# A fifth 4 KB buffer for gathered expert rows in a two-layer decoder step

## The chip, the cores and the metric

The kernel runs on one core of one Trainium2 chip. The metric is the device time of one execution in microseconds (us). Before the change it was 4011.03 us, the median of three runs (4007.59 to 4016.49).

## The reference, cut to what matters

One inference step runs two decoder layers over 512 prompt positions and 32 sample positions (8 sequences of 4). The second half of each layer is a retrieval of single-neuron experts. A product-key search gives every position 8 heads of 16 expert numbers out of 16,384 with a gate for each; the position's output is a gated sum of rows of V, weighted by a dot product with rows of U:

```
a   = einsum('td,thed->the', xb, U[ib])        # rows of U, 1024 values each
wgt = gb * gelu(a)
out = einsum('the,thed->td', wgt, V[ib])       # rows of V
x   = x + out
```

Behind it stand the residual add and the RMS norm that the next layer (or the output) begins with.

## The kernel before, in words

**Two ways to the same sum.** Positions 0 to 383 (three tiles of 128) go the dense way: TensorE computes the activation of all 128 x 128 experts, a table of gates (`make_g`, line 1421 on) zeroes those that weren't chosen, and TensorE multiplies the result with all of V in the last loop of `peer`: 128 steps, each with 18 matmuls (line 1199) into six PSUM tiles. Positions 384 to 511, and the 32 sample positions, go the sparse way, by `gather` (line 1237 on): GpSimd fetches for each of 128 partitions the row of U or V that its position chose (an indirect DMA, line 1283, 128 rows of 4 KB into one buffer `g_r`), and VectorE uses it, for U with a dot product (line 1268, output `g_junk`), for V with a multiply-add into the accumulator `g_acc` (line 1276). A layer has 160 fetches of U and 160 of V, that is 320 uses on VectorE; a layer's first 128 V uses sum into the first `g_acc`, the last 32 into the second.

**Splitting.** Matmuls in float32r need each operand as a rounded high part and a rest. For a row block of V, ScalarE makes `vh` (line 98) and VectorE `vl` (line 99); for the dense weights they make `gwh` and `gwl`, for a block of U `wh` and `wl`. Step n of the last loop can't run on TensorE before its `vh`, `vl`, `gwh`, `gwl` are there.

**What sets the order around the change.** `gather` is a generator. Each call of `next` issues one fetch and, from the `GR`-th on, one use of the row that was asked for `GR - 1` calls earlier. In `make_g` the method `spend` calls it at a steady pace (a budget of 120 calls); in the last loop lines 1216 to 1218 spread the calls that are left evenly over 122 steps, and at step 123 all that is left is called, and the buffers are given back. After that come the norm of position tile 3 (`out(3, ...)`), a selection matmul on the second accumulator (line 1232), and `out` of the other tiles. The program's order is not the engines' order: a scheduler places every instruction on its engine at build time by a timeline of its own, and each engine then works through its list strictly in turn. A fetch into `g_r` waits until the use of that buffer's row before is done.

**Names.** `GR` (line 54) is the number of `g_r` buffers; lines 1279 to 1288 are the loop of `gather`. `hh` and `hl` (lines 98, 99, 181) are the next layer's inputs; in layer 0 they lie where the gather's buffers lay.

Of the kernel before, what the change touches and what calls it, by code (L numbers as in the profile page):

```python
# [50 lines left out]
GA = 4  # L51
KEEP = 6
KJ = KEEP * GA
GR = 4
APRE = 96
ROWPRE = 120
ROWSTEP = 2.5
# [22 lines left out]
class Body:  # L80
# [1156 lines left out]
    def gather(self, l, gp, acc, last):  # L1237
# [22 lines left out]
        def use(job, r):  # L1260
            nonlocal late
            which, t, s, e, w, g = job
            if late is not None and s % TOPK == 2:
                nc.vector.tensor_mul(*late)
                late = None
            if which == 0:
                jk = gp.tile([P, D], F16, name="g_junk", bufs=1)
                ins = nc.vector.scalar_tensor_tensor(jk, r, 1.0, h2t[t], op0=OP.mult, op1=OP.mult,  # L1268
                                                     accum_out=w[:, s:s + 1])
                self.tc.keep_in_program_order(ins)  # L1270
                if s % TOPK == TOPK - 1:
                    ws = w[:, s + 1 - TOPK:s + 1]
                    nc.scalar.activation(ws, ws, AF.Gelu_apprx_tanh)
                    late = (ws, ws, g[:, s + 1 - TOPK:s + 1])
            else:
                nc.vector.scalar_tensor_tensor(acc[t], r, w[:, s:s + 1], acc[t], op0=OP.mult, op1=OP.add)  # L1276

        def run():
            for n in range(len(jobs) + GR - 1):
                if n < len(jobs):  # L1280
                    which, t, s, e, w, g = jobs[n]
                    r = gp.tile([P, D], F32, name="g_r", bufs=GR)
                    nc.gpsimd.indirect_dma_start(out=r, out_offset=None,  # L1283
                                                 in_=a["v" if which else "u_rows"].rearrange("l e d -> (l e) d"),
                                                 in_offset=bass.IndirectOffsetOnAxis(ap=e[:, s:s + 1], axis=0))
                    rows.append(r)
                if n >= GR - 1:
                    use(jobs[n - GR + 1], rows.pop(0))
                yield
# [304 lines left out]
```

## Time and profile before

| | before |
|---|---|
| median of three runs | 4011.03 us |
| the profiled execution, its time | 4018.55 us |
| its span | 4016.8 us |
| TensorE matmul busy | 3798.2 us (95%) |
| VectorE busy | 2912.1 us (72%) |
| ScalarE busy | 1586.5 us (39%) |
| GpSimd busy | 1047.8 us (26%) |
| uses of U rows (line 1268) | 320, 390.3 us |
| uses of V rows (line 1276) | 320, 409.7 us |
| fetches (line 1283), U and V | 640, 936.0 us of GpSimd |
| chain that ended last | PE 79%, DVE 7%, DMA 5%, issue 5%, POOL 2% |

PE is TensorE, DVE VectorE, ACT ScalarE, POOL GpSimd, SP the engine that issues most loads. The span is the profiled stretch; the execution's time is 1.75 us longer. The profiled execution took 7.52 us more than the median. A share of busy time is a mean over stages with different limits, so the stages are read one by one.

### The profile page before, as it was taken

Reading aid. Unit: us, or ns where it says so; the run is one execution under the profiler, and the core shown is the slowest. Engines: PE = TensorE matmul, PEld = TensorE weight load, DVE = VectorE, ACT = ScalarE, POOL = GpSimd, SP = SyncE. Lnnn points to the kernel's source line nnn. Section 1 sums busy time; section 2 is a strip of 40 time slices with the busy share of each in tenths; the row PEclk is TensorE's granted clock in tenths of the full one; section 3 lists DMA queues with packets and bytes.
Section 4 is the critical chain, followed back from the end, with each engine's and each line's share of the span. In section 5 each row is a group of like instructions: output and inputs, shape, how many; then the busy total and the mean of one; then the engine's idle time right before and its main releaser. Section 6 shows DMA issues by size and latency. Waiting matters only on the chain.

```text
span 4016.8 us, 66254 instructions
## 1 busy us (share of the span) xinstructions
PE 3798.2 (95%) x25676; PEld 3426.8 (85%) x25676; DVE 2912.1 (72%) x5823; ACT 1586.5 (39%) x2377; POOL 1047.8 (26%) x880
## 2 busy tenths in 40 slices
PE   8999999999999999999679999999989989999995
PEld 7999988998898888888569998889888978888883
DVE  5554446799997878888855434568999968788887
ACT  4532333344554333333244323333455633333332
POOL 0110000004532444443511000000242224444344
PEclk9999999999999999999889999999999999999997
DMA  7243216237799999999834421361578999999997
GB/s 257 93 139 106 68 57 230 92 101 271 294 326 361 334 344 331 343 354 335 298 119 131 134 78 60 100 214 59 179 272 303 329 341 340 350 333 339 349 323 241
DMA packets 334028, 936.55 MB, mean 233 GB/s; under 512 B 28784, under 2 KB 126448, under 8 KB 330384
## 3 DMA queue, kind: packets, MB, share of 16 engines
q1 hardware_dynamic: 232912, 527.52, 38.5%
q0 software_dynamic: 92160, 335.59, 23.3%
q10 hardware_dynamic: 8640, 69.21, 4.3%
q8 instruction: 201, 3.29, 0.3%
q14 instruction: 115, 0.94, 0.1%
HBM read 835.50 MB, written 96.70 MB: 232 GB/s over the span
## 4 chain that ended last, share of the span: by engine, by line
PE 79%; DVE 7%; DMA 5%; issue 5%; POOL 2%; ACT 1%; SPq 1%; DVEq 0%; POOLq 0%; ACTq 0%
PE mm L118 34%; PE mm L1199 16%; PE sm L1199 8%; PE sm L118 7%; DMA g_r<-v,g_e 2%; POOL g_r L1283 2%; DMA g_r<-u_rows,g_e 2%; PE mm L344 2%; PE sm L586 2%; DVE wl L99 2%; PE sm L1455 1%; PE sm L1456 1%; DVE g_junk L1268 1%; PE sm L529 1%; PE sm L1340 1%
## 5 line engine op out<-in xcount | busy, mean ns | idle before, releaser
L1283 POOL DMA_INDIRECT g_r<-u_rows,g_e x320 | 488.8, 1527 | 1434.6 <-DVE g_junk L1268 706.5
L98 ACT CAST wh<-wr 128x1024 fp32r<-128x1024 f32 (+1 forms) x464 | 466.3, 1005 | 944.0 <-PE mm L118 714.9
L99 DVE TENSOR_TENSOR wl<-wr,wh 128x1024 fp32r<-128x1024 f32 (+1 forms) x464 | 541.2, 1166 | 372.1 <-ACT wh L98 363.0
L118 PE MATMUL mm<-ah,wh 128*128 128x384 f32 (+1 forms) x1792 | 597.9, 334 | 44.1 <-ACT wh L98 23.2
L118 PE MATMUL mm<-ah,wl 128*128 128x384 f32 (+1 forms) x1792 | 595.7, 335 | 27.3 <-DVE wl L99 27.2
L118 PE MATMUL mm<-al,wh 128*128 128x384 f32 (+1 forms) x1792 | 591.4, 330 | 0.5 <-DVE al L99 0.5
L1283 POOL DMA_INDIRECT g_r<-v,g_e x320 | 447.2, 1398 | 553.1 <-DVE g_acc L1276 498.9
L1276 DVE SCALAR_TENSOR_TENSOR g_acc<-g_r,g_w,g_acc 128x1024 f32<-128x1024 f32 x320 | 409.7, 1280 | 38.0 <-DMA g_r<-v,g_e 36.0
L1268 DVE SCALAR_TENSOR_TENSOR g_junk<-g_r,h2t 128x1024 f16<-128x1024 f32 x320 | 390.3, 1220 | 28.4 <-DMA g_r<-u_rows,g_e 27.5
L118 PEld LDWEIGHTS mm<-ah,wh 128*128 128x128 f32 x1792 | 341.1, 190 | 54.6 <-ACT wh L98 24.7
L118 PEld LDWEIGHTS mm<-ah,wl 128*128 128x128 f32 x1792 | 340.6, 190 | 39.0 <-DVE wl L99 38.4
L99 DVE TENSOR_TENSOR vl<-vr,vh 128x1024 fp32r<-128x1024 f32 x256 | 312.9, 1222 | 43.7 <-ACT vh L98 43.3
L118 PEld LDWEIGHTS mm<-al,wh 128*128 128x128 f32 x1792 | 341.2, 190 | 0.9 <-DVE al L99 0.9
L118 PE MATMUL mm<-hh,wl 128*128 128x272 f32 x1536 | 333.9, 294 | 0.0
L118 PE MATMUL mm<-hl,wh 128*128 128x272 f32 x1536 | 331.2, 293 | 0.0
L118 PE MATMUL mm<-hh,wh 128*128 128x272 f32 x1536 | 329.0, 294 | 0.0
L1199 PE MATMUL mm<-vl,gwh 128*128 128x512 f32 x1024 | 317.2, 391 | 0.0
L1199 PE MATMUL mm<-vh,gwl 128*128 128x512 f32 x1024 | 316.3, 390 | 0.0
L1199 PE MATMUL mm<-vh,gwh 128*128 128x512 f32 x1024 | 278.9, 391 | 1.3 <-ACT vh L98 1.1
L98 ACT CAST vh<-vr 128x1024 fp32r<-128x1024 f32 x256 | 269.3, 1053 | 4.7 <-DMA vr<-v 4.7
L118 PEld LDWEIGHTS mm<-hl,wh 128*128 128x128 f32 x1536 | 243.2, 189 | 8.4 <-issue 6.1
L118 PEld LDWEIGHTS mm<-hh,wl 128*128 128x128 f32 x1536 | 244.6, 189 | 5.5 <-issue 2.4
(478 smaller groups left out, 7378.1 us busy)
## 6 DMA issues: line engine op xcount, KB each, us to landing
vr<-v SPq DMA_DIRECT2D x256, 512.0 KB, 6.6
wr<-u SPq DMA_DIRECT2D x240, 512.0 KB, 5.4
wr<-w_in SPq DMA_DIRECT2D x96, 512.0 KB, 3.6
gd<-stage ACTq DMA_DIRECT2D x24, 1664.0 KB, 9.2
gt<-gd SPq DMA_DIRECT2D x52, 768.0 KB, 8.1
ad<-ga ACTq DMA_DIRECT2D x36, 768.0 KB, 7.3
gr<-ad SPq DMA_DIRECT2D x36, 768.0 KB, 7.9
wr<-w_o SPq DMA_DIRECT2D x32, 512.0 KB, 3.8
```

What stands on the lines that cost most here:

```text
L98: self.nc.scalar.copy(hi, src)
L99: self.nc.vector.tensor_sub(lo, src, hi.bitcast(F32))
L118: nc.tensor.matmul(o, w[:, k * P:(k + 1) * P], x[part][:, k], start=(q == 0), stop=(q == 3 * nk - 1))
L344: nc.tensor.matmul(ps[i][s][:np_], m[:, k, c], w[:, s * 512:(s + 1) * 512], start=(k == 0 and q == 0), stop=(k == NK - 1 and q == 2))
L529: nc.tensor.matmul(ps[i], x[:, k, i * P:(i + 1) * P], w[:, kk * BW:(kk + 1) * BW], start=(k == 0 and q == 0), stop=(k == NK - 1 and q == 2))
L586: self.pairs_of(lambda b, lo, hi: nc.tensor.matmul(p[lo:hi, b], w[lo:hi, b], x(b, lo, hi), start=True, stop=True))
L1199: ins = nc.tensor.matmul(po[i][s], w[:, i * P:(i + 1) * P], v[:, s * 512:(s + 1) * 512], start=(step == 1 and m == 0), stop=(step == NKEY ...
L1268: ins = nc.vector.scalar_tensor_tensor(jk, r, 1.0, h2t[t], op0=OP.mult, op1=OP.mult, accum_out=w[:, s:s + 1])
L1276: nc.vector.scalar_tensor_tensor(acc[t], r, w[:, s:s + 1], acc[t], op0=OP.mult, op1=OP.add)
L1283: nc.gpsimd.indirect_dma_start(out=r, out_offset=None, in_=a["v" if which else "u_rows"].rearrange("l e d -> (l e) d"), in_offset=bass.Ind ...
L1340: nc.tensor.matmul(ps[:, j, half], q[:, half, (i + j) * P:(i + j + 1) * P], sub[:, h * 2 + half], start=True, stop=True)
L1455: nc.tensor.matmul(ps[:, t], p_[:, w, :, half], qh[:, w, :, half], start=True, stop=False)
```

## The change

`gather` gets five buffers in place of four. A row is then asked for four calls ahead of its use; a layer's loop in `gather` has 324 calls where it had 323.

```diff
@@ -51,7 +51,7 @@
 GA = 4
 KEEP = 6
 KJ = KEEP * GA
-GR = 4
+GR = 5
 APRE = 96
 ROWPRE = 120
 ROWSTEP = 2.5
```

`GR` stands in three places: the number of buffers (`bufs=GR`), the length of the loop (`len(jobs) + GR - 1`) and the distance of use from fetch (`n >= GR - 1`). Since the scheduler places the instructions anew, their order on the engines changes too.

VectorE at the end of layer 0, from the last steps of the last loop on. `vl` and `gwl` feed TensorE's steps, line 1276 uses a V row, `hl` is the next layer's input. Before:

```order
L99 TENSOR_TENSOR vl<-vr,vh 128x1024
L173 SCALAR_TENSOR_TENSOR gr<-g_acc_14562,rs_y,gt 128x1024
L1276 SCALAR_TENSOR_TENSOR g_acc_14563<-g_r,g_w_9484,g_acc_14563 128x1024
L99 TENSOR_TENSOR gwl<-ga,gwh 128x384
L99 TENSOR_TENSOR vl<-vr,vh 128x1024
L1276 SCALAR_TENSOR_TENSOR g_acc_14563<-g_r,g_w_9484,g_acc_14563 128x1024 x28
L99 TENSOR_TENSOR hl<-sm,hh 128x4x128 x2
```

The same place with five buffers:

```order
L99 TENSOR_TENSOR vl<-vr,vh 128x1024
L99 TENSOR_TENSOR gwl<-ga,gwh 128x384
L1276 SCALAR_TENSOR_TENSOR g_acc_14561<-g_r,g_w_9484,g_acc_14561 128x1024
L99 TENSOR_TENSOR vl<-vr,vh 128x1024
L1276 SCALAR_TENSOR_TENSOR g_acc_14561<-g_r,g_w_9484,g_acc_14561 128x1024
L99 TENSOR_TENSOR gwl<-ga,gwh 128x384
L1276 SCALAR_TENSOR_TENSOR g_acc_14561<-g_r,g_w_9484,g_acc_14561 128x1024
L99 TENSOR_TENSOR vl<-vr,vh 128x1024
L99 TENSOR_TENSOR hl<-sm,hh 128x4x128 x2
```

The 28 uses behind the layer's last `vl` are gone from there; they stand between the steps before it.

VectorE at the end of layer 1; line 156 begins the last norms. Before:

```order
L1276 SCALAR_TENSOR_TENSOR g_acc_34013<-g_r,g_w_28934,g_acc_34013 128x1024
L99 TENSOR_TENSOR gwl<-ga,gwh 128x384
L1276 SCALAR_TENSOR_TENSOR g_acc_34013<-g_r,g_w_28934,g_acc_34013 128x1024
L99 TENSOR_TENSOR vl<-vr,vh 128x1024
L1276 SCALAR_TENSOR_TENSOR g_acc_34013<-g_r,g_w_28934,g_acc_34013 128x1024 x20
L156 TENSOR_SCALAR n_v<-n_ss 32x1
```

With five buffers:

```order
L1276 SCALAR_TENSOR_TENSOR g_acc_34011<-g_r,g_w_28934,g_acc_34011 128x1024
L99 TENSOR_TENSOR gwl<-ga,gwh 128x384
L99 TENSOR_TENSOR vl<-vr,vh 128x1024
L1276 SCALAR_TENSOR_TENSOR g_acc_34011<-g_r,g_w_28934,g_acc_34011 128x1024
L156 TENSOR_SCALAR n_v<-n_ss 32x1
```

Of the 20 uses behind the last `vl` one is left.

ScalarE at the end of layer 1, where the norms of the last tiles begin (line 153 sums squares, line 134 takes the root). Before:

```order
L98 CAST vh<-vr 128x1024
L153 ACTIVATE gr,n_ss<-sm 32x512
L153 ACTIVATE gr,n_ss<-sm 128x512 x2
L153 ACTIVATE gr,n_ss<-sm 32x512
L134 ACT_TABLE_LOAD
L134 ACTIVATE rs_s<-n_v 32x1
```

With five buffers:

```order
L98 CAST vh<-vr 128x1024
L153 ACTIVATE gr,n_ss<-sm 32x512
L153 ACTIVATE gr,n_ss<-sm 128x512 x2
L153 ACTIVATE gr,n_ss<-sm 32x512
L134 ACTIVATE rs_s<-n_v 32x1
```

The table load stands earlier now, inside the last loop, with no other table behind it.

## Rows read from the trace of the kernel before

**Rows 1.** Busy time by stretch: us, PE, PEld, DVE, ACT, POOL (instructions), PEclk, DMA share, GB/s
```profile
1310.00:1972.00 662.00, 660.90 (x3065) 565.90 (x3064) 542.79 (x669) 239.74 (x327) 281.70 (x204) 1.00 0.95 338
1979.00:2025.00 46.00, 0.00 (x0) 0.00 (x0) 30.82 (x24) 0.22 (x1) 24.30 (x21) 0.54 0.76 260
3300.00:3950.00 650.00, 650.00 (x3015) 556.57 (x3014) 536.19 (x656) 236.85 (x322) 281.49 (x205) 1.00 0.94 337
3965.00:3996.00 31.00, 0.00 (x0) 0.00 (x0) 21.30 (x17) 0.00 (x0) 16.12 (x14) 0.57 0.78 262
1250.00:1300.00 50.00, 40.92 (x224) 39.55 (x222) 30.02 (x43) 17.28 (x25) 16.88 (x12) 0.90 1.04 382
```

**Rows 2.** PE's waits, 1310 to 2030 and 3300 to 3998: total us, times, longest
```profile
PE sm L1232 <- DVE hl L99: 47.4, 1, 47.4
PE mm L1199 <- ACT vh L98: 1.1, 1, 1.1
...
PE sm L1232 <- DVE g_acc L1276: 31.2, 1, 31.2
PE sm L1199 <- DVE vl L99: 1.6, 2, 1.0
```

**Rows 3.** Chain that ended last: start us, us, what; both layers' ends
```profile
2017.42 5.90 DMA g_r<-v,g_e
...
2023.42 1.30 DVE g_acc L1276
...
2024.78 0.59 ACT hh L98
...
2025.40 0.70 DVE hl L99
...
2026.14 1.93 PE sm L1232 x2
...
4000.53 1.28 ACT L134
```

**Rows 4.** DVE by line, 1979 to 2025 and 3965 to 3996: busy, mean ns, idle before
```profile
L1276 DVE SCALAR_TENSOR_TENSOR g_acc<-g_r,g_w,g_acc 128x1024 f32<-128x1024 f32 x24 | 30.8, 1284 | 15.8 <-DMA g_r<-v,g_e 15.5
...
L1276 DVE SCALAR_TENSOR_TENSOR g_acc<-g_r,g_w,g_acc 128x1024 f32<-128x1024 f32 x17 | 21.8, 1284 | 10.5 <-DMA g_r<-v,g_e 10.3
```

**Rows 5.** DVE's waits in the last loop of layer 0, 1310 to 1972
```profile
DVE gwl L99 <- ACT gwh L98: 76.6, 67, 3.3
DVE vl L99 <- ACT vh L98: 19.2, 44, 1.4
...
DVE g_junk L1268 <- DMA g_r<-u_rows,g_e: 6.0, 3, 3.1
DVE g_acc L1276 <- DMA g_r<-v,g_e: 2.1, 2, 1.4
```

**Rows 6.** DMA, 1310 to 1972: all packets, GpSimd's queue, issue to landing; then 3300 to 3950
```profile
DMA packets 89544, 224.08 MB, mean 338 GB/s; under 512 B 6499, under 2 KB 40349, under 8 KB 89501
...
q0 software_dynamic: 29231, 106.44, 43.3%
...
g_r<-v,g_e POOLq DMA_INDIRECT x136, 7.4
...
DMA packets 88174, 218.92 MB, mean 337 GB/s; under 512 B 6344, under 2 KB 40136, under 8 KB 88130
```

**Rows 7.** Waits of DVE and PE in the two `make_g` stages, 860 to 1310 and 2840 to 3300
```profile
DVE g_junk L1268 <- DMA g_r<-u_rows,g_e: 8.6, 4, 5.9
...
PE mm L118 <- DVE wl L99: 19.9, 12, 8.4
...
DVE g_junk L1268 <- DMA g_r<-u_rows,g_e: 10.5, 3, 8.9
```

**Rows 8.** Timeline of POOL: start us, us, instruction [idle before <-releaser]
```profile
1068.82 25.99 POOL L1283 DMA_INDIRECT g_r<-u_rows,g_e  x1 [3.32 <-DVE g_junk L1268]
...
1924.79 4.02 POOL L1283 DMA_INDIRECT g_r<-v,g_e  x1 [0.66 <-DVE g_acc L1276]
```

## The prediction

> **What bounds the kernel now.** I read the busy time by stretch first [rows 1]. In the last loop of `peer` TensorE is busy 660.9 of 662 us in layer 0 and 650.0 of 650 in layer 1, at the full granted clock (1.00), while VectorE is busy 542.79 and 536.19: TensorE is the bound there. In the stretch behind each loop TensorE has no instruction at all for 46 and 31 us, and VectorE is busy 30.82 and 21.30 us of them. The waits of TensorE say for whom [rows 2]: one wait of 47.4 us in layer 0 and one of 31.2 us in layer 1, both of the selection matmul (line 1232), against 1.1 and 1.6 us in the loops. In layer 0 the wait is put down to `hl`, but the chain [rows 3] shows what is ahead of it: fetch and landing of a V row, its use, then the casts `hh` and `hl` (0.59 and 0.70 us), then the matmul at 2026.14. `hh` is late because it lies where the gather's buffers lay. So both waits are for the gather's last rows. VectorE's lines in these stretches [rows 4] hold nothing but V uses, 24 and 17 of them at 1.28 us, with 15.8 and 10.5 us of waiting for rows between them. That is 46/24 = 1.92 and 31/17 = 1.82 us per row. The prize is 47.4 + 31.2 = 78.6 us in which the core does nothing but the end of the sparse path.
>
> **What the change moves.** Counting uses (lines 1268 and 1276) in VectorE's order against the first and the last `vl` of a layer, the 320 uses stood as 84 before, 208 between, 28 behind in layer 0, and 80, 220, 20 in layer 1. With five buffers they stand as 85, 235, 0 and 85, 234, 1. The pieces of order above show the ends. So 27 uses in layer 0 and 14 in layer 1 go from the empty stretch into the loops, and 1 and 5 go ahead of them. The fetches go with them, on GpSimd's own list, where only fetches stand in the loops. One more call per layer in the loop of `gather` issues and uses nothing.
>
> **The sum, step by step.**
>
> 1. The waits behind the loops. In layer 0 nothing of the gather stands behind the last `vl`; the last use ends before that `vl` begins, and the casts `hh` and `hl` (two each, 0.59 and 0.70 us) go beside the last matmuls: of the 28 uses behind the last `vl` 24 lay after 1979, so TensorE worked on for some 4 x 1.28 = 5 us after that `vl`. The wait of 47.4 us goes: -47.4. In layer 1 (3 of 20 uses, 3.8 us) the one use that is left fits beside the matmuls too: -31.2. Next in line is what already follows the selection matmul: norms, transposes, stores.
>
> 2. The table load on ScalarE, 1.28 us on the chain at 4000.53 [rows 3], now stands inside the loop, where ScalarE is busy 237 of 650 us [rows 1]: -1.3.
>
> 3. VectorE in the loops. 27 uses at 1.28 us are 34.6 us more in 662, 14 are 17.9 in 650: VectorE goes from 82% to 87% and 85%. What covers it is idle time: 119 us in layer 0, of which 76.6 are waits for `gwh` [rows 5], a cast that ScalarE makes as soon as TensorE gives its buffer back. VectorE there waits for TensorE's pace, so more work first fills these waits. If all cover were gone, the price would be 34.6 + 17.9, and 6 x 1.22 for the uses that went ahead of the loops, 59.8 us; the lower end is 0. The nearest row is the 1.6 us that TensorE waited for `vl` at the dense end of layer 1 [rows 2]; I take 2 us per layer: +4.
>
> 4. The rows' own lateness. A buffer in the loop of layer 0 came round every 4 uses, 4 x 662/208 = 12.7 us; now every 5, 5 x 662/235 = 14.1 us. A row lands 7.4 us after its issue [rows 6] and is used in 1.28, so the time to spare grows from 4.0 to 5.4 us though rows come denser. In the loop of layer 0 VectorE waits 6.0 + 2.1 us for rows now [rows 5]; bounds -8 to +8, taken as 0.
>
> 5. DMA. A fetch moves 106.44/204 = 0.522 MB [rows 1, 6]. Layer 0's loop goes from 224.08 to 238.2 MB, 360 GB/s over 662 us; layer 1's from 218.92 to 226.2 MB, 348 GB/s. The stretch from 1250 to 1300 moved 382 GB/s over 50 us [rows 1], so this fits, with landings somewhat later: 0.
>
> By the Trainium skill's page "DMA: Bandwidth & Descriptors", section Specifications, HBM gives one core about 358 GB/s; by that limit layer 0's loop would need some 665 us, 3 us more than now, and the sum would come to about -73 in place of -76. The 382 GB/s in the trace speak against it as a hard limit here.
>
> 6. The `make_g` stages, where the uses of U rows begin. In layer 0 VectorE's order there is the same up to its end; in layer 1 some uses shift by a few places. VectorE waits there 8.6 and 10.5 us for rows in all [rows 7]. A fifth buffer can take from these waits or leave them: bounds -19 to +19 (another draw of the same waits), taken as 0.
>
> Sum: -47.4 - 31.2 - 1.3 + 4 = -75.9. Against the profiled execution's own time, 4018.55, that gives 3942.7. That execution was 7.5 us above the median of the three runs; against the median, 4011.03, it gives **3935**, which I forecast.
>
> **The rivals.**
>
> *A, the feed of TensorE slips.* VectorE's list is in strict order: a use whose row is late holds the `vl` and `gwl` behind it, and these hold TensorE. For it speaks that the pairs `vh`/`vl` have two buffers only, that VectorE at 87% has fewer gaps, and the 1.6 us above; against it that TensorE waited 1.1 us in 662. The whole price of step 3 gives -79.9 + 59.8 = -20.1, about 3991; half of it -50, 3961. Chance 0.14.
>
> *B, GpSimd is locked out in the loops: slower.* One fetch in `make_g` took 25.99 us [rows 8], against a mean of 281.70/204 = 1.38 in the loop [rows 1]. GpSimd's instruction is short, so something held it, and in those stages VectorE waits up to 5.9 and 8.9 us for a row and TensorE up to 8.4 us for VectorE [rows 7]. If the cause is VectorE's density, its remaining gaps in the loops (85 of 119 us) may be too short, and such lock-outs come there; each then costs TensorE about 8.4 us. Nine eat the 75.9 us; at twelve, one in 110 us of the loops, the time is 3935 + 101 = 4036. Against it: VectorE is at 82% now, and the longest fetch in layer 0's loop took 4.02 us [rows 8]. Chance 0.03.
>
> The Trainium skill's page "SBUF — State Buffer", section "SBUF: two separate sides", has the rule behind B: a VectorE instruction with two SBUF inputs and a GpSimd instruction that reads SBUF exclude each other, and the loser is fully blocked. The 25.99 us agree with it; the loop, full of such VectorE instructions, shows no block of that length.
>
> *C, the waits in `make_g` go too.* With one row more in hand VectorE bridges the late rows: 19.1 us more, 3916. For it: these waits end on landings. Against: in a long block GpSimd stands until VectorE stops, however many rows are in hand. Chance 0.10.
>
> *D, the change doesn't do what its order says.* The order was placed on a timeline with its own landings. If the rows land so late that each use in the loops waits as in the stretches behind them, 15.8/24 = 0.66 us, the 469 uses there wait 309 us; VectorE has 119 + 114 = 233 us of idle time, and the 76 us left over take the gain back: about 4011, no change. Against it: the present loops wait 8 us for 208 rows. Chance 0.03.
>
> **How the numbers follow.** My forecast has 0.70, with 3925 to 3946 as its own spread (steps 3 to 6). The range reaches down to C with a little more, 3912, and up past half of A, 3966; outside lie the rest of A, B and D, and a corner of C. Two measurements of this kernel can be told apart from about 0.2%, 8 us. Faster by more: forecast, A and C, 0.94. Within: D, 0.03. Slower: B, 0.03.
>
> **What would show it.** In the profile after, the selection matmul (line 1232) follows the last matmul of line 1199 within 2 us in both layers, and VectorE has no run of V uses alone behind the last `vl`. The loops keep their length within some 5 us at VectorE 85 to 87% and some 350 to 360 GB/s. The norm at the end of layer 1 has no table load. Wrong would be: a loop that is longer by 15 us or more with waits of TensorE for `vl` or `gwl` (A; for DMA, step 5), fetches of over 8 us in the loops (B), waits for rows of over 0.3 us per use in the loops (D), or `make_g` stages that end more than 10 us earlier or later (step 6).

## The result and the profile after

The changed kernel takes 3960.66 us, median of 4 runs (3954.92 to 3978.91), against 4012.27 (4007.59 to 4016.49) before on the same chip: ratio 0.9879, 95% interval 0.9844 to 0.9915, 51.6 us less. The number lies in the range, 26 us above the forecast of 3935 and at the place where the first rival stood with half of its price. So the question of the experiments is where some 25 us of the forecast gain went.

The profiled execution took 3965.26 us with a span of 3963.5. Busy time by stretch, for the two loops and what stands behind them; columns as in [rows 1]:

```profile
1316.00:2005.00 689.00, 671.68 (x3094) 570.10 (x3093) 572.23 (x687) 240.30 (x329) 317.51 (x222) 1.00 0.95 341
2005.00:2025.00 20.00, 11.34 (x47) 7.70 (x46) 12.77 (x42) 13.14 (x36) 0.22 (x4) 0.68 0.25 88
3290.00:3944.00 654.00, 644.04 (x2963) 546.18 (x2962) 551.01 (x658) 229.07 (x314) 308.44 (x216) 1.00 0.95 342
```

The stretches without any matmul are gone: in the 20 us behind the loop TensorE is busy 11.34 again. But in the loops TensorE, which stood still for 1.1 us in layer 0 and not at all in layer 1 before [rows 1], now does so for 17 of 689 and 10 of 654 us. Its waits say at what, first from 1300 to 2020, then from 3260 to 3963 (total us, times, longest):

```profile
PE mm L1199 <- ACT vh L98: 8.8, 8, 1.1
PE mm L1199 <- DVE vl L99: 5.8, 3, 2.2
...
PE mm L1199 <- ACT vh L98: 5.5, 5, 1.1
...
PE mm L1199 <- DVE vl L99: 1.9, 4, 0.9
```

Line 1232 no longer appears: 47.4 and 31.2 us of waiting [rows 2] are gone. In their place stand 13 short waits of the loops for `vh` and 7 for `vl`, the two halves of the V tile, none longer than 1.1 and 2.2 us. The rest of the 17 and 10 us are two waits of 1.3 us in each layer for `ga`, an activation that ScalarE makes between the casts.

A stage table needs marks that all kernels have. The view of one source line gives for each form of matmul its count, shortest, median and longest duration in ns, and the start of the first and the last. The kernel before, both layers:

```profile
L1199 PE MATMUL mm<-vh,gwh x512: 389/389/501, 1308.8 to 1977.5; 128*128 128x512 f32 x171
...
L1199 PE MATMUL mm<-vh,gwh x512: 387/389/502, 3294.8 to 3963.7; 128*128 128x512 f32 x171
```

After:

```profile
L1199 PE MATMUL mm<-vh,gwh x512: 387/389/502, 1314.5 to 2004.8; 128*128 128x512 f32 x171
L1232 PE MATMUL sm<-g_acc,kc x4: 592/604/617, 2005.8 to 2007.6; 128*32 128x512 f32 x4
...
L1199 PE MATMUL mm<-vh,gwh x512: 389/389/498, 3264.0 to 3943.6; 128*128 128x512 f32 x171
L1232 PE MATMUL sm<-g_acc,kc x4: 592/592/617, 3944.8 to 3946.1; 128*32 128x512 f32 x4
```

The matmul kept its median of 389 ns; and the selection matmul starts 1.0 and 1.2 us after the last matmul of the loop. From these marks, us (the later kernels are those of the experiments; spans and marks of one profiled execution each):

```
                            to loop 0   loop 0   between   loop 1   to the end   span
before                        1308.8     668.7    1317.3    668.9      53.1     4016.8
after                         1314.5     690.3    1259.2    679.6      19.9     3963.5
after, once more              1319.7     690.2    1248.9    678.9      19.9     3957.6
five buffers, three ahead     1318.8     690.2    1254.6    679.0      19.8     3962.4
four, feed in order           1311.1     667.3    1316.4    663.5      55.8     4014.1
five, feed in order           1315.0     678.0    1262.0    670.9      19.8     3945.7
five, feed in order, again    1315.2     677.9    1264.3    671.3      19.9     3948.6
five, narrow V uses           1306.3     671.2    1262.4    667.6      19.9     3927.4
five, feed, third gwh         1311.4     677.0    1252.2    675.0      20.1     3935.7
five, feed, gwh and gwl x3    1311.5     670.4    1268.9    667.2      19.9     3937.9
```

Before to after: +5.7 + 21.6 - 58.1 + 10.7 - 33.2 = -53.3 us, which is the difference of the spans. The parts behind the loops gave what was forecast (78.6 + 1.3 = 79.9) and some 11 us more; the two loops took 32.3 back where 4 had been allowed. A program's own scatter shows in the rows "after", "once more" and "three ahead", whose lists of instructions are all but the same: the loops agree to 0.7 us, the stretch between them to 10 us only.

### The profile page after: what moved, and what is told of

The parts are those of the page before. It is cut to its first block, busy times and chain, and to the rows that moved or that the text cites. A ratio compares the mean times of both kernels' runs of the same rounds, so it can differ in the third digit from the quotient of the medians.

```text
span 3963.5 us, 66227 instructions
## 1 busy us (share of the span) xinstructions
PE 3799.7 (96%) x25676; PEld 3421.2 (86%) x25676; DVE 2910.4 (73%) x5823; ACT 1580.6 (40%) x2374; POOL 1081.4 (27%) x880
## 4 chain that ended last, share of the span: by engine, by line
PE 83%; DVE 7%; issue 3%; DMA 3%; ACT 2%; POOL 1%; SPq 0%; DVEq 0%; POOLq 0%; ACTq 0%
PE mm L118 36%; PE mm L1199 17%; PE sm L1199 8%; PE sm L118 7%; DMA g_r<-u_rows,g_e 2%; PE mm L344 2%; PE sm L586 2%; DVE wl L99 2%; PE sm L1456 1%; PE sm L1455 1%; DVE g_junk L1268 1%; POOL g_r L1283 1%; PE sm L529 1%; PE sm L1340 1%; ACT wh L98 0%
## 5 line engine op out<-in xcount | busy, mean ns | idle before, releaser
L1283 POOL DMA_INDIRECT g_r<-u_rows,g_e x320 | 503.6, 1574 | 1387.5 <-DVE g_junk L1268 678.5
L1283 POOL DMA_INDIRECT g_r<-v,g_e x320 | 465.8, 1456 | 495.2 <-DVE g_acc L1276 437.9
L98 ACT CAST gwh<-gr 128x384 fp32r<-128x384 f32 x144 | 74.0, 514 | 445.2 <-PE sm L1199 442.6
```

Source lines behind the costliest of these rows:

```text
L98: self.nc.scalar.copy(hi, src)
L1283: nc.gpsimd.indirect_dma_start(out=r, out_offset=None, in_=a["v" if which else "u_rows"].rearrange("l e d -> (l e) d"), in_offset=bass.Ind ...
```

## What the loops wait for

The place of one stall, on ScalarE's timeline of the changed kernel (start us, duration, instruction, and in brackets the idle time before it with its releaser):

```profile
1929.70 1.06 ACT L98 CAST vh<-vr 128x1024 fp32r<-128x1024 f32 x1
1933.33 0.52 ACT L98 CAST gwh<-ga 128x384 fp32r<-128x384 f32 x1 [2.57 <-PE sm L1199]
1937.41 0.51 ACT L98 CAST gwh<-ga 128x384 fp32r<-128x384 f32 x1 [3.56 <-PE sm L1199]
1937.83 1.99 ACT L98 CAST vh<-vr 128x1024 fp32r<-128x1024 f32 x2
```

VectorE in the same place:

```profile
1937.96 0.56 DVE L99 TENSOR_TENSOR gwl<-ga,gwh 128x384 fp32r<-128x384 f32 x1 [1.00 <-ACT gwh L98]
1938.43 1.96 DVE L1178 TENSOR_TENSOR gr<-gr,gt 128x384 f32<-128x384 f32 x4
1940.31 1.28 DVE L1276 SCALAR_TENSOR_TENSOR g_acc<-g_r,g_w,g_acc 128x1024 f32<-128x1024 f32 x1
1941.51 1.22 DVE L99 TENSOR_TENSOR vl<-vr,vh 128x1024 fp32r<-128x1024 f32 x1
```

And TensorE:

```profile
1938.92 1.19 PE L1199 MATMUL mm<-vh,gwh 128*128 128x512 f32 x4 [1.10 <-ACT vh L98]
...
1942.78 0.73 PE L1199 MATMUL mm<-vl,gwh 128*128 128x512 f32 x2 [2.20 <-DVE vl L99]
```

Read it from the first cast. At 1933.33 ScalarE casts `gwh` of a step. The normal next cast is `vh` of the same step, as at 1929.70. Here the scheduler has put `gwh` of the step after it first. There are two buffers for `gwh`, so that cast must wait until TensorE has finished the step before, 3.56 us in ScalarE's list; only then, from 1937.83, both `vh` are cast. But TensorE, having finished that step, needs the first `vh` at once: it stands for the length of that cast, 1.10 us. VectorE could make `vl` from 1938.9 on, but its list has the `gwl` of the step after, four products (line 1178) and a V use ahead of it, so `vl` starts at 1941.51, and TensorE stands 2.20 us more. On both engines one instruction stands in front of the wrong other; VectorE has no idle time between its four rows here, so its fuller list adds to the second wait.

Counted in the engines' lists, `gwh` stands ahead of the `vh` of the step before it at 3 steps of layer 0 and 2 of layer 1 in the kernel before, and at 15 and 12 steps in the changed one. In the kernel before the one such place late in the loop is the one wait of 1.1 us of [rows 2]; in the changed one the 8 and 5 waits for `vh` stand at such steps, and so do six of the seven waits for `vl`. Theories: **order**, that these reversals cost the 25 us; **density**, that VectorE's higher load does; **rows**, that rows come late with the denser uses.

## The experiments

The first four ran on one chip (before: 4010.83 us, median of 17). Two short pieces of code recur. "Feed in order" keeps, on ScalarE and VectorE, the casts `gwh` and `gwl` of a step behind `vh` and `vl` of the step before; it only fixes the order of the lists and adds no wait (`behind` is a dependency without a semaphore). Line 1199 becomes 1204 by it:

```diff
-        self.nc.scalar.copy(hi, src)
-        self.nc.vector.tensor_sub(lo, src, hi.bitcast(F32))
+        return self.nc.scalar.copy(hi, src), self.nc.vector.tensor_sub(lo, src, hi.bitcast(F32))
...
-                        self.split(wh, wl, ga)
+                        for now, was in zip(self.split(wh, wl, ga), fed):
+                            self.behind(now, was)
...
-                        self.split(vh, vl, vr)
+                        fed = self.split(vh, vl, vr)
```

"Rows in order" keeps `gwl` of a step behind the last V or U use that the program has ahead of it, so that the uses are drawn into the loop without a fifth buffer:

```diff
+                        if step and self.used is not None:
+                            self.behind(made[1], self.used)
```

**The change once more.** No edit.

> The change as it is, once more, beside the kernels it is compared with. Both theories: 3955 to 3975 us, TensorE's waits for vh and vl in the two loops 15 us in layer 0 and 7 in layer 1, at the same steps as in the first profile of it.

Measured 3958.22 us (3947.61 to 3977.75), ratio 0.9865 (0.9842 to 0.9889). The result stands.

**Five buffers, feed in order.**

> Five buffers; in the last loop each gwh and gwl stands behind the vh and vl of the step before, as the program has it. Theory order (the missing 25 us went to the places where the scheduler put gwh of a step ahead of vh of the step before): TensorE's waits for vh and vl in the loops fall under 4 us in both layers together, the time falls by 20 to 30 us against the plain change, to about 3935. Theory density (VectorE at 83 to 87% is too full to feed TensorE): the waits stay at 15 and 7 us or move to vl, the time stays within 8 us of the plain change.

Measured 3946.13 us (3936.86 to 3947.5), ratio 0.9827 (0.981 to 0.9845), 12 us below the plain change beside it. Its loops are 12.3 and 8.7 us shorter than after's, and the waits for `vh` fall from 8.8 to 3.3 us in layer 0 and from 5.5 to none in layer 1; those for `vl`, 5.8 and 1.9 us in the changed kernel, stay (layer 0, then layer 1):

```profile
PE mm L1204 <- DVE vl L98: 5.0, 6, 1.4
PE mm L1204 <- ACT vh L98: 3.3, 3, 1.3
...
PE mm L1204 <- DVE vl L98: 3.4, 5, 1.2
```

The waits that are left come to 11.7 us, not to under 4, and the time falls by 12 us, not by 20 to 30. So the order is a cause, worth 21 us in the loops, but not the only one. Less than 21 us arrives at the end, which is taken up below.

**Four buffers, feed in order.**

> Four buffers, with the same rule for gwh and gwl. VectorE's list still has 28 and 20 uses of rows behind the last vl. Both theories of the loss: TensorE still waits some 47 and 31 us for the gather behind its loops, the time is that of the kernel before less 0 to 5 us, about 4009. If the rule itself were worth 20 us with four buffers too, it would not be the extra reversals of the change that the rule removes.

Measured 4010.71 us, ratio 0.9991 (0.9973 to 1.0009): no change, and the waits behind the loops stand as before:

```profile
PE sm L1237 <- DVE hl L98: 46.4, 1, 46.4
...
PE sm L1237 <- DVE g_acc L1281: 33.9, 1, 33.9
```

The order of the feed alone takes nothing from the tails. Beside the kernel with five buffers it also gives the loops' length with no reversal and no more uses than before: 667.3 and 663.5 us. In layer 1 the marks enclose 3070 matmuls in place of 3090, so only layer 0's length compares with the others.

**Four buffers, rows and feed in order.**

> Four buffers, gwh and gwl behind the vh and vl of the step before, and gwl also behind the uses of V rows that the program has ahead of it, so that no use is left behind the last vl. Theory placement (the chip needs the uses to stand inside the loop, not the fifth buffer): the waits of 47 and 31 us go, rows are late by little, 3930 to 3950 us. Theory buffer (with four buffers rows come too late for that place: about 10.8 us round trip against 7.4 to land and 1.3 to use): VectorE waits 50 us or more for rows in the loops, TensorE waits for gwl, 3970 to 4010 us.

Measured 3992.52 us (3976.96 to 4002.36), ratio 0.9947 (0.9926 to 0.9968). The waits behind the loops are gone, but this stands in the loop of layer 0, and 34.2 us in that of layer 1:

```profile
PE mm L1207 <- DVE gwl L98: 37.5, 4, 29.3
```

The one stall of 29.3 us stands at the loop's start: in VectorE's list 124 uses are ahead of the fifth `vl` in place of 97, because the program issues its uses ahead of where the scheduler had put them, and the edit moves all of that backlog ahead of the first steps. Rows are late in it too: from 1362 to 1391.3, inside the stall, VectorE waits

```profile
DVE g_junk L1277 <- DMA g_r<-u_rows,g_e: 10.4, 8, 2.6
```

So this kernel doesn't tell whether four buffers would do; the next but one was made to avoid the pile.

**Five buffers, asked for three steps ahead.** The next three and this one shared a chip on which the kernel before took 4015.19 us (median of 11), so ratios are compared. Against the changed kernel:

```diff
-GR = 5
+GR = 4
...
-                    r = gp.tile([P, D], F32, name="g_r", bufs=GR)
+                    r = gp.tile([P, D], F32, name="g_r", bufs=GR + 1)
```

> Five buffers, but the call that asks for a row stands three steps ahead of its use as in the kernel before. In the loops GpSimd's list holds only fetches, each of which waits for its buffer, and the engines' lists are the changed kernel's to within a few places (no V use behind the last vl of layer 0, one of layer 1). If the gain is the buffer's, this is the plain change again: 3958 us, within 8. If the extra step of asking ahead is what brings it, the waits behind the loops (47 and 31 us) come back and the time is near 4011.

Measured 3965.5 us, ratio 0.9879 (0.986 to 0.9898): the plain change again, down to TensorE's waits in layer 0's loop (8.8 us for `vh`, 5.8 us for `vl`).

It is the buffer that acts, not the step at which the program asks.

**Four buffers, rows in order without the pile.**

```diff
-                        if step and self.used is not None:
-                            self.behind(made[1], self.used)
+                        lag = max(0, 32 * (110 - step) // 110)
+                        if len(self.used) > lag:
+                            self.behind(made[1], self.used[-1 - lag])
```

> Four buffers as before, the feed's casts in order, and gwl of a step kept behind a V use that the program has ahead of it, 32 uses back at the loop's start and none from step 110 on, so that 321 uses stand ahead of the last vl with no pile at the loop's start. If the place of the uses in VectorE's list is all that the fifth buffer brought, the stalls of 29 us at the start of the loops that the last such kernel had go, and 3992 falls by 55 to 65 us, to about 3930 to 3937, below five buffers with the feed in order (3946). If four buffers bring the rows too late for such an order, VectorE waits some 29 us for rows in layer 0's loop as in that kernel, the vl and gwl behind these uses hold TensorE, and the time stays above 3950.

Measured 3979.82 us (3973.92 to 3990.53), ratio 0.9922 (0.9901 to 0.9942): slower than five buffers with or without the feed in order. Layer 0, waits of TensorE and of VectorE:

```profile
PE mm L1208 <- DVE gwl L98: 29.0, 13, 4.4
...
DVE g_acc L1286 <- DMA g_r<-v,g_e: 18.3, 16, 3.1
...
DVE g_junk L1278 <- DMA g_r<-u_rows,g_e: 5.6, 3, 2.2
```

With four buffers and all uses in the loop VectorE waits 24 us for rows, where the changed kernel's waits for none in layer 0, and TensorE waits 29 us for `gwl` (23.1 in layer 1). The time came out as the expectation's second case has it, but the trace doesn't show its mechanism: in the 6 us ahead of each of layer 0's 13 waits for `gwl` VectorE waits for no row, and in layer 1 only two of ten waits have one ahead (2.1 and 0.3 us). The longest in layer 0, on VectorE and then on TensorE:

```profile
1776.04 1.97 DVE L1182 TENSOR_TENSOR ga<-ga,gt 128x384 f32<-128x384 f32 x4 [0.58 <-DMA gt<-gd]
1777.92 1.22 DVE L98 TENSOR_TENSOR vl<-vr,vh 128x1024 fp32r<-128x1024 f32 x1
1779.06 2.60 DVE L1286 SCALAR_TENSOR_TENSOR g_acc<-g_r,g_w,g_acc 128x1024 f32<-128x1024 f32 x2
1781.57 0.55 DVE L98 TENSOR_TENSOR gwl<-ga,gwh 128x384 fp32r<-128x384 f32 x1
...
1782.18 2.08 PE L1208 MATMUL mm<-vh,gwl 128*128 128x512 f32 x4 [4.40 <-DVE gwl L98]
```

VectorE works through from 1776.04 on; `gwl` is late because products, `vl` and two V uses stand ahead of it, and the edit itself keeps it behind uses. So what TensorE waits for in this kernel's loops is again the order of VectorE's list and its load, not a late row, and whether four buffers would do with a better list stays open. What stands is that the scheduler left 28 and 20 uses behind the loops with four buffers and 0 and 1 with five, and that VectorE waits for rows in layer 0's loop with four and not with five. As the cause of the changed kernel's own loss, late rows are excluded by that.

**Five buffers, feed in order, narrow V uses.** Each V use adds 512 of the 1024 columns of its row; half of the sparse sum is left out.

> Five buffers with the feed in order, and each V use adds only 512 of the 1024 columns of its row (the other half of the sparse sum is left out), so some 235 uses per loop take about 0.65 instead of 1.28 us; the fetches are the same. Loops, first to last matmul of line 1204's first form: 678.0 and 670.9 us with five buffers and the feed in order, 667.3 and 663.5 with four. If what is left of the loss is VectorE's load, the loops fall to about 665 in each layer and the time from 3946 to about 3930; if it is the transfers, the loops stay at 678 and 671 and the time at 3946, within 5.

Measured 3936.11 us (3928.23 to 3939.76), ratio 0.9809 (0.9789 to 0.983). The loops came to 671.2 and 667.6 us and the waits for `vl` are gone; what is left is one wait in each layer:

```profile
PE mm L1204 <- ACT vh L98: 2.3, 1, 2.3
...
PE mm L1204 <- ACT vh L98: 1.2, 1, 1.2
```

The transfers are the same, so they are not what TensorE loses to: 353 GB/s over 659 us here, without such waits. VectorE's load is part of it. The ratio's interval overlaps that of the full uses, so the verdict rests on the loops.

**Five buffers, feed in order, third buffer for `gwh`.**

```diff
-                        wh = dn.tile([P, ND], F32R, name="gwh", bufs=2)
+                        wh = dn.tile([P, ND], F32R, name="gwh", bufs=3)
```

> Five buffers with the feed in order, and a third buffer for gwh, so that this cast no longer waits for TensorE to finish the step before the last. If what is left of the loss is that vh and, behind it, vl stand on ScalarE and VectorE behind a cast that waits for TensorE, TensorE's waits for vh (3.3 us in layer 0) go and those for vl (5.0 and 3.4) shrink: about 3938. gwl keeps two buffers, so VectorE can still be held by it: then only the waits for vh go, 3943. If neither counts, 3946.

Measured 3944.24 us (3937.53 to 3947.61), ratio 0.9831 (0.9811 to 0.985): no difference to the feed in order alone. In layer 0 the waits for `vh` fall to 1.2 us; those for `vl` stay at 4.7 and rise to 5.5 in layer 1. The reason stands in VectorE's waits there:

```profile
DVE gwl L98 <- PE sm L1204: 59.3, 58, 3.4
```

VectorE stood for `gwh` before and stands for `gwl`'s own buffer now, as long as before (57.9 us): the expectation's second case.

**Uses ahead of the loop, with two and with three `gwh` and `gwl`.** The product of a U use is written over its row. Together with the feed in order this also moves 31 uses from each loop into `make_g`, by the lists (116 uses ahead of the first `vl` in place of 85). It ran beside the feed in order once more (before: 4014.79 us).

```diff
-                jk = gp.tile([P, D], F16, name="g_junk", bufs=1)
-                ins = nc.vector.scalar_tensor_tensor(jk, r, 1.0, h2t[t], op0=OP.mult, op1=OP.mult,
+                ins = nc.vector.scalar_tensor_tensor(r, r, 1.0, h2t[t], op0=OP.mult, op1=OP.mult,
```

> The kernel with five buffers and the feed in order once more, on the chip of the two kernels that run beside it: 3946 us, within 8 (ratio 0.983).

> Five buffers, the feed in order, and the product of a U use written over its row in place of a buffer of its own; by the lists 31 more uses then stand ahead of each last loop, in make_g, and the loops have about 204 as in the kernel before. If VectorE's load in the loops is what costs TensorE, the loops fall from 678 and 671 us to about 667 and 664. But VectorE is busy 289 of 305 us in make_g, so 31 uses of 1.22 us, 38 us, find 16 us of idle time there and the stage grows by some 22 us in each layer: 3946 + 44 - 18 = about 3972. If make_g's VectorE work can slip beside TensorE's without holding it, only the gain is left: 3928.

> As the kernel with the uses ahead of the loop, and gwh and gwl with three buffers each, so that neither cast waits for TensorE to finish the step before the last; vh and vl keep two. If VectorE's standing at gwl (58 us in layer 0's loop with five buffers and the feed in order) is what makes vl late, TensorE's waits for vl go and the loops come out 3 to 8 us below that kernel's. If VectorE then stands at vl instead, for the same TensorE, nothing changes: the same time within 3 us.

Measured: feed in order 3941.75 us, ratio 0.9817 (0.9801 to 0.9834); uses ahead 3998.14, ratio 0.9952 (0.9936 to 0.9969); with three pairs 3984.21, ratio 0.992 (0.9902 to 0.9937). The uses ahead of the loop cost more than the 22 us a layer that I had worked out: from 970 to 1275 VectorE is busy 297.30 of 305 us and TensorE 277.65, where it is busy 292.32 with the feed in order alone, and the first matmul of the loop starts at 1365.0, not 1315. The loops take 656.9 and 654.4 us, but their marks enclose some 100 matmuls less (2997 and 2980 in place of 3098 and 3090), so these lengths don't compare with those of the feed in order. The waits do: those for `vh` are gone, those for `vl` stay with 31 uses less, which speaks against load alone. Three pairs did take them away, and with the same marks the loops are 3.7 and 4.4 us shorter (653.2 and 650.0), as expected. TensorE's waits for the feed, layer 0 then layer 1, with two pairs:

```profile
PE mm L1204 <- DVE vl L98: 5.1, 6, 1.5
...
PE mm L1204 <- DVE vl L98: 4.1, 6, 0.9
```

and with three:

```profile
PE mm L1204 <- DVE vl L98: 0.6, 2, 0.3
PE mm L1204 <- ACT vh L98: 0.5, 1, 0.5
...
PE mm L1204 <- ACT vh L98: 0.6, 1, 0.6
```

**Five buffers, feed in order, three `gwh` and three `gwl`.** Both tiles with `bufs=3`, U uses as in the changed kernel (before: 4005.76 us).

> Five buffers, the feed in order, and gwh and gwl with three buffers each; 85 uses stand ahead of the first vl of layer 0 as with the feed in order alone, 3 or 4 behind the last vl. If VectorE's and ScalarE's standing at gwl and gwh, for TensorE to finish the step before the last, is what makes vl late, TensorE's waits for vl and vh in the loops (5.0 + 3.2 and 3.4 us with the feed in order) fall below 1.5 us as they did with the uses ahead of the loop, the loops from 678 and 671 us to about 668 and 666, and the time from 3944 to about 3930. If VectorE's 85% of load alone is the cause, the waits and the time stay, 3944 within 5; and the uses left at the end could then cost some 4 us per layer.

Measured 3937.87 us (3923.91 to 3950.41), ratio 0.9824 (0.9802 to 0.9847). The loops are as expected, 7.6 and 3.7 us shorter than with two pairs:

```profile
L1204 PE MATMUL mm<-vh,gwh x512: 387/389/504, 1311.5 to 1981.9; 128*128 128x512 f32 x171
...
L1204 PE MATMUL mm<-vh,gwh x512: 388/389/502, 3250.8 to 3918.0; 128*128 128x512 f32 x171
```

with 2.7 us of waiting for `vl` in layer 0, more than the 1.5 expected, and 1.1 for `vh` in layer 1. VectorE is busy 568.27 of 670.4 us there, 85%, so that load by itself does not hold TensorE. The ratio isn't as expected: it can't be told from the 0.9827 and 0.9817 of two pairs. The loops show the cause; a gain in time over two pairs is not shown.

**Where the loops' gain went.** With the feed in order the loops are 21 us shorter than after's, and the time 12. In the table the stretch between the loops is longer in four of the five executions with five buffers and the feed in order, 1262 to 1269 us against 1249 to 1259 in the changed kernel's three lines; the one with a third `gwh` has 1252.2. TensorE is not idle longer there (50 to 57 us in all of them). It is busy longer with the same matmuls, some 9583: 1212 us in both executions of the feed in order and with three pairs, 1207 with narrow V uses, 1200 with a third `gwh`, 1198 to 1205 in the changed kernel's. Windows on TensorE (us, busy, granted clock, DMA share, GB/s) some 250 us behind the loop of layer 0, first the changed kernel once more, where the clock stays up:

```profile
2260.00:2310.00 50.00, 50.00 (x533) 1.00 0.39 141
```

then five buffers with the feed in order, again:

```profile
2243.00:2293.00 50.00, 50.00 (x384) 0.76 0.39 138
```

and with three pairs:

```profile
2250.00:2300.00 50.00, 50.00 (x437) 0.76 0.32 113
```

and with a third `gwh` alone:

```profile
2238.00:2288.00 50.00, 49.15 (x501) 0.97 0.42 146
```

TensorE is busy nearly all the time in each, but at a mean granted clock of 0.76 it is partly at 1.2 GHz, and 0.24 x 50 = 12 us of work are lost. That is the size of what the loops' gain lost on the way to the end. The order of the feed doesn't bring this fall by itself: the kernel with a third `gwh` has that order and not the fall. And of the five runs of the feed in order the fastest, 3936.86 us, is the one with the highest mean clock, 0.988 against 0.984 to 0.986. So it seems to come in some executions and not in others; why the clock falls there stays open.

## Why the prediction was right or wrong

**Step 1, the waits behind the loops: right.** 47.4 and 31.2 us are gone, and line 1232 follows line 1199 within 1.2 us. The stretch between the loops fell by 58.1; the 10.7 above the forecast are as much as that stretch scatters between executions of the same lists, and I don't split them.

**Step 2, the table load: right.** It stands at 3906.22 now, inside the loop; the end fell by 33.2 us against 31.2 + 1.3.

**Step 3, VectorE in the loops: this is the term that was mis-sized.** I took +4 with bounds of 0 and 59.8; it measured +21.6 and +10.7, 32.3. By differences of the loops in the table, layer 0 and layer 1: the reversed casts 12.3 and 8.7 (after less feed in order); standing at `gwl` and `gwh` for TensorE's buffers 7.6 and 3.7 (two pairs less three); 1.7 and -1.7 are left to before. Two sentences of that step failed. One was "more work first fills these waits": VectorE's waits for `gwh` in layer 0's loop, 76.6 us before [rows 5], are the same after 27 uses were added:

```profile
DVE gwl L99 <- ACT gwh L98: 76.7, 65, 3.0
```

An engine with a list in strict order can't work while it stands at `gwl`; the uses behind it wait too and then run when `vl` is due. In this list the waits were not cover. In a better one much of them is: with nearly the same uses, VectorE is idle 106 us in layer 0's loop with the feed in order and 102 with three pairs, against 117 in the changed kernel, and 120 before with 27 uses less. The other was that 1.6 us at the dense end of layer 1 is the nearest row: it came from a list with 3 and 2 reversals, and the change made it 15 and 12. The lists told this ahead of any run; I compared only the places of the uses in them, not those of the casts they were put between.

**Steps 4 and 5: right.** VectorE waits for no row in layer 0's loop and 2.5 us in layer 1's; 234.65 MB move in layer 0's loop, 341 GB/s. With the same rows to fetch, three pairs bring the loops back to 670.4 and 667.2 us, before 668.7 and 668.9, so at most some 3 us in layer 0, against the 667.3 of four buffers with the feed in order, are left for the transfers to have cost. The page "DMA: Bandwidth & Descriptors" (the Trainium skill, section Specifications), with its some 358 GB/s, is not tested by this: no loop here asked for more than 353 over its length.

**Step 6, `make_g`: right within its bounds.** VectorE waits 9.0 and 9.2 us there for rows, 8.6 and 10.5 before [rows 7]; loop 0 starts 5.7 us later, 10 to 11 in the two executions with the same lists. In the profiled execution after TensorE is idle 6.4 us longer up to there; in the one called "once more" it is idle as long as before, but the same matmuls keep it busy 1260.1 us in place of 1249.7, at a granted clock of 0.98 in place of 0.99. So in that one it is not the order of `make_g` that moved the loop's start.

**The rivals.** *A* is what happened, at some half of its price, 3961; its mechanism, a strict list that holds `vl` and TensorE behind it, is the right one, but what stood ahead was a cast that waits for TensorE and not, as I had it, a use whose row is late. That second form shows only at the loops' start with four buffers and rows in order, where VectorE waits 10.4 us for rows within the stall of 29.3. At 0.14 the chance was too low, and the forecast's own spread, 3925 to 3946, missed: that the time lies in the stated range is due to the range's reaching past half of *A*, and not to the +4. Of the signs named ahead, the selection matmul and the table load came as forecast; the loops did not keep their length within 5 us, VectorE is at 83 and 84% and the transfers at 341 and 342 GB/s in them, below what was named, and the sign given for *A*, a loop longer by 15 us with TensorE waiting for VectorE's half, came in layer 0, with more of the waiting for ScalarE's. *B* didn't occur: the longest fetches in the loops took 2.89 and 4.88 us. In `make_g` there was one long fetch per layer:

```profile
972.78 30.74 POOL L1283 DMA_INDIRECT g_r<-u_rows,g_e  x1 [5.82 <-DVE g_junk L1268]
2922.47 30.76 POOL L1283 DMA_INDIRECT g_r<-u_rows,g_e  x1 [5.81 <-DVE g_junk L1268]
```

and TensorE waited 6.6 us (one wait of 6.4) and 6.4 us behind them, about the 8.4 that I had taken for one. The changed kernel's second execution had no fetch over 6 us, with the same list. This fits the rule of the page "SBUF — State Buffer" (the Trainium skill, "SBUF: two separate sides") that of the two the loser is fully blocked, and shows that whether a long block comes is not fixed by the list. *C* and *D*: no, by the waits in `make_g` and by the waits for rows in the loops.

Of the versions tried, five buffers with the feed in order are the best that is shown: 3946 and 3942 us in two sets of runs, ratios 0.9827 and 0.9817, below the changed kernel's 0.9865; the first interval, on the same chip, still touches that one's lower end (0.9845 and 0.9842), the second lies below it.

## What to carry to other kernels

When an order is made by a scheduler, a change to one buffer moves instructions that have nothing to do with it. Compare the whole list of every engine that feeds the bound, and look for an instruction that waits for the bounding engine standing ahead of one that this engine needs next. Idle time of an engine with a strict list is cover only if the added work can stand where the idle time is; a wait at a double buffer can't be filled by what is queued behind it. Judge such an edit in its own stage: a stage can be repeated to 1 us where the whole time scatters by 10.

## What was not expected of the hardware

The same short waits can cost more than their length or not. After the 1.10 and 2.20 us at 1938 and 1942 the granted clock of TensorE fell and came back within 4 us:

```profile
1943.30:1947.10 3.80, 3.80 (x11) 0.58 1.08 339
1947.20:1951.00 3.80, 3.80 (x18) 0.98 1.02 388
```

In the first 3.8 us 11 matmuls were done, in the next 18: 0.42 x 3.8 = 1.6 us lost behind 3.3 us of waiting. Behind the same two waits at 1855 and 1859, in the same loop, it did not fall:

```profile
1859.00:1863.00 4.00, 4.00 (x18) 1.00 1.04 335
```

And the fall to 0.76 for 50 us in a stage in which TensorE had no gap, seen above, is as large as more than half of what the better order won in the loops, and came in some executions only.
